# A hybrid attention layer in float32: weight splits in quarters, sums behind the value they delay, and two reorderings

## The chip, the cores and the metric

The kernel runs on one core of a Trainium2 chip (trn2). The metric is the device time of one launch in microseconds. The median of three runs is given, and one more execution was taken with the hardware profiler.

## The reference

One encoder layer on an input of 1024 tokens by 1024 features, all in float32:

```python
x = x + 0.5 * post1(SwiGLU_1(pre1(x)))                 # D_FF = 2816
h = mix_pre(x);  q, k, v = split(h @ w_qkv)            # 16 heads of 64
o_na  = neighbourhood_attention(q[:8], k[:8], v[:8])   # 16 x 64 token grid, window 8 x 16, learned bias
o_dil = dilated_mixture(q[8:], k[8:], v[8:])           # windows (128,1), (512,4), (2048,16), merged by their softmax sums
x = x + mix_post(concat(norm(o_na), norm(o_dil)) @ w_out)
x = x + 0.5 * post2(SwiGLU_2(pre2(x)))
# pre, post, norm: RMSNorm with a gain;  SwiGLU(h) = (silu(h @ w_gate) * (h @ w_up)) @ w_down
```

## The kernel before

**Precision.** Every float32 operand of a large matmul is split into two parts: `hi`, a copy cast to the matmul type fp32r by ScalarE, and `lo`, the float32 operand less `hi`, by VectorE. A product is then three matmuls: hi times hi, hi times lo and lo times hi. A matmul reads a stationary operand of 128x128 and streams a moving one of 512 columns into one of eight PSUM banks (2 KB per partition).

**Fewer products.** The GEMMs are done in a Strassen-Winograd form, seven products in place of eight, on sums and differences of blocks of the operands. The names A11, A12, S1 to S4, A22 stand for blocks or sums of the left operand, B11, B21, T1 to T4, B22 for those of the right one.

**The stages in order.** FFN1 (gate and up as pairs of columns in `PairGemm`, then the down projection in `Passes`); the projection of v (`Passes`) and of q and k (`PairGemm`); four pairs of dilated heads (`DilPair`, pairs 4 to 7); four pairs of neighbourhood heads (`na_head`); the output projection (`nat_mm`); FFN2, built as FFN1.

**PairGemm.run** goes over blocks of weights b. In an early block, whose first two products were made before, it computes S2 with T2 (and adds the stored `s1`, giving `u2`, L601), then the last product of the block before (A22), then S1 with T1 (adding u2 gives `v`, L609), S3 with T1 into another bank `d` (adding v gives `c22`, L628), and S4 with B22, which accumulates onto the bank of S1 that v has just read. The weights of block b + 1 are prepared beside it by the four steps of `prepare(b + 1)`: `direct` forms the sums and differences of the raw weights (L553, L554), `second` splits T2 (L456 on ScalarE, L457 on VectorE), `sums` splits T1 and forms one more difference (L561), and `rest` splits B22 and fetches the raw weights of block b + 3. `mm` is the product itself (L466, L467: hi with hi and lo; L472: lo with hi).

**Passes.run** goes over seven passes. `fetch` loads raw operands and splits them (L746 on ScalarE, L747 on VectorE, first the left side where it isn't resident in SBUF, then the right); L779 issues the matmuls of a product, for two blocks at a time in the first row tile and one at a time in the others.

**DilPair.head** goes over a head's four quads, each two units (eight units a head). A unit is four score matmuls (L1159), two reductions of scores plus bias by VectorE (L1066), two exponentials by ScalarE (L1068), and later the transposes of the unit three back (L1076), the copy of these into SBUF (`pt`, L1078, on VectorE or ScalarE by turns) and the products with the values of the unit four back (L1180). In the heads of pairs 6 and 7 the split of one tile of output weights of 1024 columns is put between (`Weights.steps`, L127 on ScalarE and L128 on VectorE). Its last part asks SyncE's queue for the next raw tile (`fetch`), of which there are two buffers.

**GroupNorm** normalizes the heads' outputs: `scaled(i)` multiplies one row block by its reciprocal root and the gain (L1342), `put(i)` transposes it (L1353, into one of two PSUM tiles) and splits it in two halves (L1357, L1358). The eight puts of the neighbourhood heads ("strip") go between the matmuls of the first stretch of the output projection.

**What sets the order.** TensorE runs in the order in which the program is written. On the other engines a planner orders the instructions by its own costs, those written first having precedence among those that are ready; an instruction issued inside `behind(f, engines)` comes after the last one written so far for each engine named. Each engine runs its instructions strictly in the planned order and waits for semaphores of other engines.

Of the kernel before, what the change touches and what calls it, by code (L numbers as in the profile page):

```python
# [16 lines left out]
SP, POOL, DVE, ACT = [getattr(mybir.EngineType, e) for e in ("SP", "Pool", "DVE", "Activation")]  # L17
# [7 lines left out]
NP = 4  # L25
# [160 lines left out]
class Operand:  # L186
# [10 lines left out]
    def second(self):  # L197
        for b in (S1, S2, S3, S4, A22):
            self.x[b] = [self.c.xb.tile([P, 4, T], F32R, tag=f"x{b}{i}", name=f"x{b}{i}") for i in range(2)]
# [232 lines left out]
class PairGemm:  # L432
# [151 lines left out]
    def run(self, final=None):  # L584

        c, nc, sp = self.c, self.c.nc, self.c.sp
        last = None
        if self.s1 is None:
            self.load_first()
        for b in range(self.n):  # L590
            w, early = self.w.pop(b), b < self.early
            direct, second, sums, rest = self.prepare(b + 1)
            if early:
                s1 = self.s1
                if b:
                    s1 = sp.tile([P, T], F32, tag="s1", name="s1")
                    nc.sync.dma_start(s1, self.kept[b])
                a = self.bank()
                self.mm(a, w[T2], 0, S2)
                u2 = sp.tile([P, T], F32, tag="u2", name="u2")  # L600
                nc.vector.tensor_add(u2, a, s1)  # L601
                if last:
                    last()
                self.c.behind(direct, *(self.sink.ties if b else (DVE,)))
                second()
                a = self.bank()
                self.mm(a, w[T1], 0, S1)
                v = sp.tile([P, T], F32, tag="v", name="v")
                nc.vector.tensor_add(v, a, u2)  # L609
            else:  # L610
                a = self.bank()
                self.mm(a, w["g"], 0, A11)
                s1 = self.keep(a, "s1")
                if last:
                    last()
                self.mm(a, w[T2], 0, S2, True)
                u2 = self.keep(a, "u2")
                pb = self.bank()
                self.mm(pb, w["g"], 1, A12)
                self.sink.first(b, pb, False, s1)  # L620
                self.tied(direct)
                second()
                self.mm(a, w[T1], 0, S1, True)
                v = self.keep(a, "v")
            d = self.bank()
            self.mm(d, w[T1], 1, S3)
            c22 = c.cp.tile([P, T], F32, tag="g2", name="c22", bufs=self.sink.deep)
            nc.vector.tensor_add(c22, d, v)  # L628
            self.sink.third(b, c22)
            sums()  # L630
            self.mm(a, w[B22], 0, S4, True)
            if final and b == self.n - 1 and self.sink.soon:
                final = final()
                c.behind(lambda: self.sink.second(b, a, u2 if early else None), DVE)
            else:
                self.sink.second(b, a, u2 if early else None)

            def last(b=b, d=d, w=w, u2=u2, c22=c22, rest=rest):
                self.mm(d, w[B22], 1, A22, True)
                c21 = c.cp.tile([P, T], F32, tag="c", name="c21")  # L640
                c.behind(lambda: nc.vector.tensor_add(c21, d, u2), *((DVE,) if self.sink.soon and b == self.n - 1 else ()))  # L641
                rest()
                self.sink.last(b, c21, c22, final)
            c.tick()
        if not self.sink.soon:
            final()
        last()
# [68 lines left out]
class Passes:  # L716
# [39 lines left out]
    def run(self, *which, upto=6):  # L756

        c = self.c
        for p in which:
            chained = PASSES[p][0] in CHAINED  # L760
            if not chained:
                self.acc = [None] * 4
            acc, groups = self.acc, self.groups[p]
            for gi, g in enumerate(groups):
                self.fetched(len(g) + 1, upto)
                ops = [self.ready.popleft() for _ in g]
                end = gi == len(groups) - 1
                for t in range(4):
                    if t == 1:
                        self.fetched(3, upto)  # L770
                    if acc[t] is None:
                        acc[t] = c.psm.tile([P, T], F32, tag="mm", name="accp")
                    sl = slice(t * P, (t + 1) * P)
                    n = 2 if t == 0 else 1
                    for j in range(0, len(ops), n):
                        two = [(a[:, sl], b) for i in (0, 1, 2) for (ahi, alo), (bhi, blo) in ops[j:j + n]
                               for a, b in [((ahi, bhi), (ahi, blo), (alo, bhi))[i]]]
                        for i, (a, b) in enumerate(two):
                            c.nc.tensor.matmul(acc[t], a, b, start=not chained and gi == 0 and j == i == 0,  # L779
                                               stop=end and j + n >= len(ops) and i == len(two) - 1,  # L780
                                               skip_group_check=chained)
                        if n == 2 or j % 2:
                            c.step()
                    if end:
                        self.take(p, t, acc[t])
                    c.tick()
# [295 lines left out]
class DilPair:  # L1082
# [28 lines left out]
    def head(self, hd, st, q, g, late, parts=(1, 0), more=(), begun=0):  # L1111
        more = deque(more)
        for i, (part, quad) in enumerate((part, quad) for part in parts for quad in range(2)):
            if (part, quad) == (0, 1):
                late()
            if i >= begun:
                self.quad(hd, st, q, g, part, quad, mid=(more, 1 - i) if i < 2 and more else ())

    def begin(self, st, g):

# [240 lines left out]
def layer(tc, a, out):  # L1361
    nc = tc.nc
    c = Ctx(tc)
    with ExitStack() as ctx:
# [10 lines left out]
        def ordered(*more):  # L1375
            return tc.manual_schedule(engines={mybir.EngineType.PE, *more})
# [464 lines left out]
        early = []  # L1841
# [8 lines left out]
        with ordered():  # L1850
            ops = sub()
            c.op = pool("op", 2, ops)
            c.vp.append(c.op)

            def next_ready():

                if loaded:
                    d, st, g = loaded[0]
                    if isinstance(d, DilPair):
                        qs.append(q_by_residue(c, nc.gpsimd.tensor_copy, st))  # L1860
                        by_residue(nc.gpsimd.tensor_copy, g[:, 0], g[:, 2])
            for p in range(NP, 2 * NP):
                for hd in range(2):
                    d, st, g = next_head(2 * (p - NP) + hd)
                    if (p, hd) == (NP + 1, 0):
                        queued(lambda: [c.w.fetch() for _ in range(2)] + [load_gains()])
                    if hd == 0:
                        d.outputs()
                    d.head(hd, st, qs.popleft(), g, next_ready, (1, 0) if p > NP or hd else (0, 1),
                           c.w.steps(2) if p > NP + 1 else (), (p, hd) == (NP, 0))  # L1870
            c.left = 64
            for p in range(NP):
                for hd in range(2):
                    vs, st, nb = next_head(8 + 2 * p + hd)
                    if (p, hd) == (NP - 1, 1):
                        c.todo.append(most)
                    na_head(c, p, hd, og[0], vs, st, nb, next_ready, last if (p, hd) == (NP - 1, 1) else lambda q: None)
            c.last_units()
            c.fill(len(c.fillers))
            c.tick(len(c.todo))  # L1880
            on = [c.xt.tile([P, 2, 4, T], F32R, tag=f"o{h}", name=f"n{h}") for h in (0, 2)]
            puts = deque()
            for quad, n in enumerate(early):
                n.ot = on
                for i in range(4):
                    if quad and i < 3:
                        puts.append(lambda i=i, n=n: (c.behind(lambda: n.scaled(i + 1), DVE), n.put(i)))
                    elif not quad and i == 0:
                        puts.append(lambda n=n: (n.put(0), c.behind(lambda: early[1].scale(1), DVE)))
                    else:  # L1890
                        puts.append(lambda i=i, n=n: n.put(i))
        s5.close()
# [3 lines left out]
        with ordered():  # L1896
            part, ws, od = [xo[k] for k in ("part", "ws", "dil")]
# [112 lines left out]
```

## Time and profile before

| | |
|---|---|
| Median of 3 runs | 1836.84 us (1836.69 to 1837.46) |
| Profiled execution | 1835.18 us |
| Its span, first to last instruction | 1833.0 us |
| Granted TensorE clock, mean | 0.999 |
| Busy: TensorE, VectorE, ScalarE, GpSimdE | 1813.7, 1321.5, 836.4, 324.1 us |
| Share of the chain that ended last | TensorE 93%, VectorE 3%, ScalarE 1%, DMA 1% |

In a row of the timeline the columns are the start in us, the duration in us, the engine, the line of the kernel, the operation, the tile written and those read, the count of instructions merged, and in brackets how long the engine stood idle before it and what ended the wait. In the view of waits they are the total in us, the number of waits and the longest. In the groups by line the two numbers behind the first bar are the busy time in us and the mean duration of one in ns, and behind the second bar the idle time before. Matmuls overlap, so their durations add up to more than the time that passes; TensorE's pace is read from the differences of its starts. PE is TensorE, DVE VectorE, ACT ScalarE, POOL GpSimdE, SP SyncE.

### The profile page before, as it was taken

To read this page: it belongs to the slowest core of one execution; us is meant where nothing else is said; L and a number is where in the kernel's file an instruction comes from. 1 tells how busy PE (TensorE), PEld (TensorE's weight loads), DVE (VectorE), ACT (ScalarE), POOL (GpSimd) and SP (SyncE) were. 2 spreads that over 40 slices of the span, in tenths; PEclk is the share of its full clock that TensorE was granted. 3 is DMA by queue.
4 is the path that set the end of the run, shared out by engine and by line. 5 is a ranking of instruction groups with operands and counts; after the bars stand their busy time and mean duration, and the time that the engine had idled before them with its cause. 6 is when DMAs were issued, how large, how long until landed. Compare 5 with 4: busy or idle time off the path is not lost.

```text
span 1833.0 us, 25132 instructions
## 1 busy us (share of the span) xinstructions
PE 1813.7 (99%) x8904; PEld 1525.8 (83%) x8904; DVE 1321.5 (72%) x2243; ACT 836.4 (46%) x1479; POOL 324.1 (18%) x508
## 2 busy tenths in 40 slices
PE   8999999999999999999999999999999999999998
PEld 6887888888888888888999998888888888888886
DVE  6878876776466877578677856788887777654557
ACT  6622233334444656234788765564223333354433
POOL 2123111112021133132333100121111111110000
PEclk9999999999999999999999999999999999999999
DMA  7756466557888868778686523594555566596564
GB/s 282 266 173 219 160 227 222 203 207 263 311 302 299 287 206 269 254 232 291 195 285 217 189 101 107 185 317 167 191 170 208 188 226 223 184 339 211 189 229 146
DMA packets 172991, 409.66 MB, mean 223 GB/s; under 512 B 20081, under 2 KB 42513, under 8 KB 170818
## 3 DMA queue, kind: packets, MB, share of 16 engines
q1 hardware_dynamic: 124706, 246.33, 40.6%
q0 software_dynamic: 47152, 159.64, 23.9%
q10 hardware_dynamic: 1008, 2.10, 0.3%
q8 instruction: 70, 1.15, 0.3%
q14 instruction: 55, 0.45, 0.1%
HBM read 280.49 MB, written 132.56 MB: 225 GB/s over the span
## 4 chain that ended last, share of the span: by engine, by line
PE 93%; DVE 3%; ACT 1%; issue 1%; DMA 1%; POOL 0%; SPq 0%; DVEq 0%; POOLq 0%; ACTq 0%
PE accp L779 27%; PE mmp L467 17%; PE mmp L466 17%; PE mmp L472 17%; PE po L1180 2%; PE po L1293 2%; PE ptp L1076 2%; PE accp L357 1%; PE accp L359 1%; PE accp L358 1%; PE trp L174 1%; PE sp L1277 1%; PE sp L1159 1%; ACT pb L1068 1%; DVE pt L1078 0%
## 5 line engine op out<-in xcount | busy, mean ns | idle before, releaser
L466 PE MATMUL mmp<-x,whi 128*128 128x512 f32 (+1 forms) x1464 | 571.9, 391 | 2.3 <-ACT x L181 1.3
L467 PE MATMUL mmp<-x,whi 128*128 128x512 f32 (+1 forms) x1464 | 569.7, 389 | 0.7 <-DVE x L182 0.6
L779 PE MATMUL accp<-pw 128*128 128x512 f32 x1800 | 411.0, 390 | 0.0
L779 PEld LDWEIGHTS accp<-pw 128*128 128x128 f32 x1800 | 337.3, 188 | 69.7
L472 PE MATMUL mmp<-x,wlo 128*128 128x512 f32 (+1 forms) x1464 | 390.5, 389 | 0.0
L466 PEld LDWEIGHTS mmp<-x,whi 128*128 128x128 f32 x1464 | 275.6, 188 | 60.8 <-ACT x L181 2.2
L467 PEld LDWEIGHTS mmp<-x,whi 128*128 128x128 f32 x1464 | 275.8, 188 | 57.3 <-DVE x L182 1.5
L472 PEld LDWEIGHTS mmp<-x,wlo 128*128 128x128 f32 x1464 | 274.6, 188 | 56.6
L747 DVE TENSOR_TENSOR pw<-praw,pw 128x1024 fp32r<-128x1024 f32 (+1 forms) x181 | 199.7, 1144 | 125.0 <-ACT pw L746 124.3
L746 ACT CAST pw<-praw 128x1024 fp32r<-128x1024 f32 (+1 forms) x181 | 168.5, 982 | 207.6 <-PE accp L779 165.6
L456 ACT CAST whi<-wraw 128x1024 fp32r<-128x1024 f32 x126 | 132.6, 1052 | 179.7 <-PE mmp L467 165.3
L457 DVE TENSOR_TENSOR wlo<-wraw,whi 128x1024 fp32r<-128x1024 f32 x126 | 153.9, 1223 | 2.7 <-ACT whi L456 2.7
L689 POOL DMA_DIRECT2D g<-sg x44 | 23.9, 543 | 430.8 <-DVE sg L682 243.0
L456 ACT CAST whi<-traw 128x512 fp32r<-128x512 f32 x52 | 32.3, 620 | 134.7 <-DVE traw L554 83.2
L641 DVE TENSOR_TENSOR c<-mmp,u 128x512 f32<-128x512 f32 x52 | 36.0, 692 | 76.6 <-PE mmp L472 76.4
L481 ACT COPY s<-mmp 128x512 f32<-128x512 f32 x52 | 30.6, 588 | 131.4 <-PE mmp L472 121.3
L553 DVE TENSOR_TENSOR wraw<-wraw 128x1024 f32<-128x1024 f32 x52 | 63.6, 1224 | 12.6 <-DMA wraw<-in_wu_dram 11.8
L779 PE MATMUL accp<-pw,x 128*128 128x512 f32 x312 | 72.0, 391 | 0.4 <-DVE pw L747 0.4
L779 PEld LDWEIGHTS accp<-pw,x 128*128 128x128 f32 x312 | 58.4, 188 | 12.9 <-DVE pw L747 0.8
L628 DVE TENSOR_TENSOR c<-mmp,v 128x512 f32<-128x512 f32 x52 | 35.8, 689 | 36.9 <-PE mmp L472 31.7
L1293 PE MATMUL po<-vs,pt 128*128 128x128 f32 x352 | 49.9, 276 | 0.0
L1076 PE MATMUL ptp<-ident,pb 128*128 128x128 f32 x304 | 48.8, 272 | 0.0
(273 smaller groups left out, 2489.0 us busy)
## 6 DMA issues: line engine op xcount, KB each, us to landing
praw<-g SPq DMA_DIRECT2D x70, 512.0 KB, 5.6
wraw<-in_wg_dram SPq DMA_DIRECT2D x44, 512.0 KB, 4.2
wraw<-in_wu_dram SPq DMA_DIRECT2D x44, 512.0 KB, 7.2
tr<-in_wd_dram SPq DMA_DIRECT2D x44, 512.0 KB, 6.8
g<-sg POOLq DMA_DIRECT2D x88, 256.0 KB, 5.2
ts<-tr POOLq DMA_DIRECT2D x22, 1024.0 KB, 4.7
praw<-ts SPq DMA_DIRECT2D x88, 256.0 KB, 4.0
praw<-in_wd_dram SPq DMA_DIRECT2D x66, 256.0 KB, 5.9
```

Source lines behind the costliest of these rows:

```text
L456: nc.scalar.copy(hi, raw)
L457: nc.vector.tensor_sub(lo, raw, hi.bitcast(F32))
L466: mm(out, hi[:, i, sl], xhi[:, k, cols], start=not go_on and k == 0, stop=False, skip_group_check=go_on)
L467: mm(out, hi[:, i, sl], xlo[:, k, cols], start=False, stop=False, skip_group_check=go_on)
L472: mm(out, lo[:, i, sl], xhi[:, k, cols], start=False, stop=k == 3, skip_group_check=go_on)
L553: nc.vector.tensor_sub(r[:, 0:2], r[:, 1:3], r[:, 0:2])
L746: nc.scalar.copy(hi, raw[:, :m])
L747: nc.vector.tensor_sub(lo, raw[:, :m], hi.bitcast(F32))
L779: c.nc.tensor.matmul(acc[t], a, b, start=not chained and gi == 0 and j == i == 0, stop=end and j + n >= len(ops) and i == len(two) - 1, sk ...
L1076: nc.tensor.transpose(ps[:, j, :], src[:, j * P:(j + 1) * P], c.ident)
L1180: nc.tensor.matmul(po[:, un * 2 + j], pt[:, 2 * j + t, :], rhs, start=t == 0, stop=t == 1)
L1293: nc.tensor.matmul(po[0][:, u], pt[0][:, j, :], vs[:, k0 + j, :], start=j == 0, stop=j == n - 1)
```

## The change

Four edits. In `PairGemm.run`, for the first block only, the steps `direct` and `second` of the second block are written behind v, and `direct` is ordered behind v's instruction on VectorE; before, they were written ahead of the product S1, `direct` ordered behind what VectorE had then. In `Passes.run` the three matmuls of a product go hi-hi, lo-hi, hi-lo (left part named first) instead of hi-hi, hi-lo, lo-hi. In `DilPair.head` the split of a weight tile goes in four parts of 256 columns, one to each quad (ahead of units 1, 2, 5 and 6), instead of two parts of 512 to the first two quads (ahead of units 1 and 2). In the output projection's puts the second quad's first two scalings are done at once, behind the first quad's first put, and the third and fourth each a put earlier.

```diff
                 if last:
                     last()
-                self.c.behind(direct, *(self.sink.ties if b else (DVE,)))
-                second()
+                if b:
+                    self.tied(direct)
+                    second()
                 a = self.bank()
                 self.mm(a, w[T1], 0, S1)
                 v = sp.tile([P, T], F32, tag="v", name="v")
                 nc.vector.tensor_add(v, a, u2)
+                if not b:
+                    self.c.behind(direct, DVE)
+                    second()
...
-                               for a, b in [((ahi, bhi), (ahi, blo), (alo, bhi))[i]]]
+                               for a, b in [((ahi, bhi), (alo, bhi), (ahi, blo))[i]]]
...
-                self.quad(hd, st, q, g, part, quad, mid=(more, 1 - i) if i < 2 and more else ())
+                self.quad(hd, st, q, g, part, quad, mid=(more, (i + 1) % 2) if more else ())
...
-                           c.w.steps(2) if p > NP + 1 else (), (p, hd) == (NP, 0))
+                           c.w.steps(4) if p > NP + 1 else (), (p, hd) == (NP, 0))
...
                 for i in range(4):
-                    if quad and i < 3:
-                        puts.append(lambda i=i, n=n: (c.behind(lambda: n.scaled(i + 1), DVE), n.put(i)))
+                    if quad and i < 2:
+                        puts.append(lambda i=i, n=n: (c.behind(lambda: n.scaled(i + 2), DVE), n.put(i)))
                     elif not quad and i == 0:
-                        puts.append(lambda n=n: (n.put(0), c.behind(lambda: early[1].scale(1), DVE)))
+                        puts.append(lambda n=n: (n.put(0), c.behind(lambda: early[1].scale(2), DVE)))
```

## The prediction, made before the changed kernel was run

> **What bounds the kernel now.** I read the page first: the span and TensorE's share of it.
>
> ```profile
> span 1833.0 us, 25132 instructions
> PE 1813.7 (99%) x8904; PEld 1525.8 (83%) x8904; DVE 1321.5 (72%) x2243; ACT 836.4 (46%) x1479; POOL 324.1 (18%) x508
> ```
>
> TensorE is busy for all but 19.3 us, most of that at the two ends. No edit takes a matmul away, so the only thing to gain is time in which TensorE stands still, and the only way to lose is to make it stand longer. The view of the waits on TensorE's side names where it stands away from the ends:
>
> ```profile
> PE mmp L466 <- DVE v L609: 1.0, 1, 1.0
> PE trp L1353 <- DVE og L1342: 0.9, 2, 0.5
> PE po L1180 <- DVE pt L1078: 0.7, 3, 0.3
> PE po L1180 <- ACT s L1068: 0.6, 2, 0.3
> PE accp L779 <- DVE pw L747: 0.4, 1, 0.4
> ```
>
> Each of the four edits meets one of these (the two rows of po L1180 are one place). They add up to only 3.6 us, but a wait also empties the pipeline of matmuls, so I measured each place by the spacing of TensorE's own starts, in the timeline, and those losses are larger.
>
> **Dilated heads' splits in four parts.** The starts of six consecutive heads:
>
> ```profile
> 929.71 0.72 PE L1159 MATMUL sp<-st,q 128*128 128x256 f32 x4
> 944.16 0.72 PE L1159 MATMUL sp<-st,q 128*128 128x256 f32 x4
> 959.25 0.37 PE L1159 MATMUL sp<-st,q 128*128 128x256 f32 x1
> 974.64 0.72 PE L1159 MATMUL sp<-st,q 128*128 128x256 f32 x4
> 989.73 0.72 PE L1159 MATMUL sp<-st,q 128*128 128x256 f32 x4
> 1005.13 0.48 PE L1277 MATMUL sp<-st 128*128 128x256 f32 x2
> ```
>
> The head from 929.71 has no split in it and takes 14.45 us (eight units of 1.81). The four after it each carry one split of a weight tile in two halves and take 15.09, 15.39, 15.09 and 15.40: 0.64 + 0.94 + 0.64 + 0.95 = 3.17 us of loss. How a half makes the loss, in the second of them:
>
> ```profile
> 961.76 0.60 ACT L127 CAST whi<-wraw 128x512 fp32r<-128x512 f32 x1
> 962.51 0.68 DVE L128 TENSOR_TENSOR wlo<-wraw,whi 128x512 fp32r<-128x512 f32 x1
> 963.12 0.42 DVE L1066 CUSTOM_DVE_ANT_0 s<-sp,g 128x256 f32<-128x256 f32 x1
> 963.46 0.69 DVE L1078 COPY pt<-ptp 128x512 f32<-128x512 f32 x1
> 964.29 1.13 PE L1180 MATMUL po<-va,pt 128*128 128x128 f32 x8 [0.28 <-ACT s L1068]
> ```
>
> VectorE runs without a hole from the split's subtraction L128 through a softmax's reduction L1066 to the copy pt, and pt ends at 964.15, just ahead of the product that reads it (the ScalarE instruction that the row names was long done). The half at the next unit does the same again: two stalls a head, 0.32 us each in the heads that lost 0.64 and 0.47 in those that lost 0.95. A quarter is 256 columns wide. The nearest rows of that width:
>
> ```profile
> L1358 DVE TENSOR_TENSOR n<-trp,n 128x256 fp32r<-128x256 f32 x16 | 6.7, 422 | 2.4 <-ACT n L1357 2.4
> L1357 ACT CAST n<-trp 128x256 fp32r<-128x256 f32 x16 | 5.7, 374 | 11.5 <-DVE n L1358 6.6 <-PE trp L1353 4.8
> ```
>
> So a quarter's subtraction takes 0.42 instead of 0.68, and pt comes 0.26 us earlier at each stall: 0.06 and 0.21 are left of 0.32 and 0.47. Four stalls of each kind: 4 x (0.06 + 0.21) = 1.08 left, 2.09 gained. The other two quarters go to units 5 and 6 of the head, where so far there is no split. VectorE has room there:
>
> ```profile
> 969.99 0.42 DVE L1066 CUSTOM_DVE_ANT_1 s<-sp,g 128x256 f32<-128x256 f32 x1 [0.92 <-PE sp L1159]
> 973.60 0.42 DVE L1066 CUSTOM_DVE_ANT_1 s<-sp,g 128x256 f32<-128x256 f32 x1 [0.93 <-PE sp L1159]
> ```
>
> It stood idle for 0.92 us before unit 5's reductions and 0.93 before unit 7's, waiting for TensorE's scores; two quarters need 0.84. I take them as hidden there. If they are not, they cost up to 8 x (0.37 + 0.42) = 6.3 us, ScalarE's cast and VectorE's subtraction one behind the other; if everything fits, the gain is the full 3.17. The fetch that follows a split goes out on SyncE's queue with the last part, some four units (7.2 us) later than now; the tile is wanted a head (15 us) on, and what then stands ahead of it in that queue are loads for the next pair, which come earlier for it. I cost it at nothing; a landing late by more than 7 us would stall the next split.
>
> By the rows, 1024 columns cost ScalarE 4 x 0.37 = 1.5 us in quarters against 2 x 0.60 = 1.2 in halves, and VectorE 4 x 0.42 = 1.7 against 2 x 0.68 = 1.4; what counts is that each piece is shorter where it stands in the way. The Trainium skill, "VectorE: DVE Perf Modes", section on the TRN2 errata, says that both engines pay a fixed latency per instruction and advises tiles of at least 512 elements, which halves keep and quarters break; from its formulas I would estimate 0.40 us for a quarter's cast and 0.42 for its subtraction. The trace agrees with these sizes, so the sum is the same by either; only the advice says otherwise, and what it would mean here is the second rival.
>
> **Left low products ahead of right.** One place shows a wait:
>
> ```profile
> 726.67 0.61 PE L779 MATMUL accp<-pw,x 128*128 128x512 f32 x2
> 727.66 2.14 PE L779 MATMUL accp<-pw,x 128*128 128x512 f32 x8 [0.38 <-DVE pw L747]
> 444.45 174.80 PE accp L779 x771
> 1266.93 0.91 PE mmp L472 x4
> ```
>
> The third matmul was due 2 x 0.227 behind 726.67, at 727.12, and came at 727.66: 0.54 lost to the weights' low half. With the operand's low half multiplied first, four matmuls stand ahead of it and it is due at 727.58: 0.08 is left, 0.46 gained. The order also breaks pairs of matmuls that share their stationary operand. The third row has 771 matmuls of which two in three share: 0.2267 us each. The fourth has four with an operand each: 0.2275. The difference would be 0.6 us over these 771 and some 1.7 over all of L779's, which are about three times as many, but the starts are rounded to 0.01; I take zero and keep 1.7 for the range.
>
> **Sums of the second block's weights behind v.** This acts in the first block of each of the three paired GEMMs. In the last one, FFN2:
>
> ```profile
> 1260.84 0.68 DVE L601 TENSOR_TENSOR u<-mmp,s 128x512 f32<-128x512 f32 x1
> 1261.44 1.22 DVE L553 TENSOR_TENSOR wraw<-wraw 128x1024 f32<-128x1024 f32 x1
> 1262.69 0.69 DVE L554 TENSOR_TENSOR traw<-wraw 128x512 f32<-128x512 f32 x1
> 1262.81 1.07 PE L472 MATMUL mmp<-x,wlo 128*128 128x512 f32 x4
> 1263.49 0.62 ACT L456 CAST whi<-traw 128x512 fp32r<-128x512 f32 x1 [3.83 <-DVE traw L554]
> 1264.02 0.68 DVE L609 TENSOR_TENSOR v<-mmp,u 128x512 f32<-128x512 f32 x1
> 1264.85 0.47 PE L466 MATMUL mmp<-x,whi 128*128 128x512 f32 x1 [0.97 <-DVE v L609]
> 1267.68 0.39 PE L466 MATMUL mmp<-x,whi 128*128 128x512 f32 x1
> ```
>
> The product S4 adds onto the bank that holds S1's, and v reads that bank in between, so S4 waits for v. The row at 1262.81 closes S3; a product of 12 matmuls takes 2.72 us, so S3 ended at 1263.72 and S1 at 1261.00. v could have run behind u at 1261.44; instead L553, L554 and L561 stood ahead of it. S4 should have begun at 1263.72 and ended at 1266.44; it ended at 1267.68: 1.24 us lost. With the sums behind v, v ends near 1262.1 and S4 finds it done: the whole 1.24, which I round to 1.2. What is queued behind v now: L553 from 1262.1, L554 at 1263.3, ScalarE's cast of T2 at 1264.0 instead of 1263.49, its low half by 1265.4. The next block's first product wants T2 at 1266.44, so a margin of a microsecond stays. In the other two GEMMs v was in time:
>
> ```profile
> 787.90 0.68 DVE L609 TENSOR_TENSOR v<-mmp,u 128x512 f32<-128x512 f32 x1
> 789.94 0.39 PE L466 MATMUL mmp<-x,whi 128*128 128x512 f32 x1
> ```
>
> In the q/k GEMM S4 begins at 789.94, S1 ended two products' starts earlier, at 787.22. There the edit only makes the sums wait: v at 787.3, then 1.22 + 0.69 + 0.62 + 0.69 of sum, difference, cast and low half: T2 ready near 791.3 where the next block begins one product behind 789.94, at 792.66. FFN1 has the same order and margin. I take no cost; without that margin it would be up to 1 us in each.
>
> **Strip norm's scalings one put ahead.** In the output projection's first stretch:
>
> ```profile
> 1126.50 0.63 PE L1353 MATMUL trp<-ident,og 128*128 128x128 f32 x4 [0.41 <-DVE og L1342]
> 1130.29 0.42 DVE L1358 TENSOR_TENSOR n<-trp,n 128x256 fp32r<-128x256 f32 x1 [0.44 <-ACT n L1357]
> 1130.63 0.74 DVE L1342 SCALAR_TENSOR_TENSOR og<-og,y,gd 128x512 f32<-128x512 f32 x1
> 1131.52 0.63 PE L1353 MATMUL trp<-ident,og 128*128 128x128 f32 x4 [0.53 <-DVE og L1342]
> ```
>
> The wait at 1126.50 is for the first scaling, which is as late as before. That at 1131.52 is for the fourth (1130.63 to 1131.37), which now comes a put earlier. But then L1358 of the put before is what is late: a put's transposes take one of two PSUM tiles, freed only by the second L1358 of the put two back, and a scaling of 0.74 moved ahead of it pushes 1130.71 to about 1131.2. So 0.2 to 0.6 of the 0.53 and its refill comes back; I take 0.3, and -0.2 as the bad end.
>
> **The sum.** 2.1 + 1.2 + 0.5 + 0.3 = 4.1 us. Nothing behind these places can swallow it: from the FFN2 start to the end TensorE's starts run at their spacing, so what is gained there and before moves the end. The profiled execution took 1835.18 us, 2.18 beyond its span; the runs' median is 1836.84. The profile should fall to about 1831.1, the median to 1832.7.
>
> **The rivals.**
> First, the quarters give back what they gain: ScalarE is busy with the units' exponentials, so a cast comes behind them, the in-order VectorE stands at L128, and new stalls as long as the remaining ones (1.1 us) appear there; or one of the small edits yields nothing. The gain is then 4.1 - 1.1 = 3.0, down to 1.9: 1834.4, within 0.2% of before (3.7 us, about what a measurement of this kernel can tell from no change). For it: each piece pays its fixed cost again. Against: the idle 0.92 and 0.93.
> Second, slower. The old stalls stay, because the pieces' order on VectorE and not their length made them, and all eight new quarters are exposed at 0.37 + 0.42 in units 5 and 6: 6.3 - 2.0 from the other edits = 4.3 slower, 1841.1. It decides if VectorE's idle time there falls before the cast is done rather than after. The Trainium skill's advice against tiles under 512 elements ("VectorE: DVE Perf Modes", same section) speaks for this one.
> Third, the sums behind v do not do what they say: T2 of the second block comes late in FFN2 and the wait moves from S4 to the next product: 1.2 less, 1833.9.
>
> **How the numbers follow.** Forecast 0.62 (own range 1830.5 to 1833.1), first rival 0.20, third 0.10, second 0.08. Faster by over 0.2% is the forecast: 0.62. Within: 0.20 + 0.10 = 0.30. Slower: 0.08. The low end of the range is every loss recovered, 3.17 + 1.24 + 0.54 + 0.9 or so, less a remainder: 1830.5; the high end leaves out only the second rival: 1837.0.
>
> **What would show it.** Right: heads of about 14.7 us between 944 and 1005; no wait on v L609 in FFN2, with v directly behind u; the wait on pw L747 under 0.1; four L127 and four L128 of 256 columns in each of the four heads. Wrong: new waits of po L1180 in the second half of those heads; a wait of mmp on a cast or low half of T2 in a second block; a mean spacing of L779's matmuls over 0.227; DVE og L1342 or a PSUM tile still holding the last put by 0.5.

## The result, and the profile after

The changed kernel takes 1832.60 us (median of 19 runs, 1831.38 to 1835.54) where the kernel before, run beside it, takes 1836.51 (19 runs, 1835.64 to 1838.58). The ratio is 0.9979, with a 95% interval of 0.9973 to 0.9985: faster by 3.9 us, 0.21% (2.8 to 5.0 us by the interval). The profiled execution took 1833.65 us. (Four lines were added to the file ahead of the loops, so that L779 is L783 in the rows below, L609 is L610, L1180 is L1184, and so on; L127 and L128 stand where they stood.)

The head of the page after, and from the view of TensorE's waits the rows that answer to those of before:

```profile
span 1831.5 us, 25146 instructions
PE 1814.0 (99%) x8904; PEld 1526.9 (83%) x8904; DVE 1321.9 (72%) x2251; ACT 835.6 (46%) x1487; POOL 322.5 (18%) x508
...
PE po L1184 <- DVE pt L1082: 0.8, 3, 0.3
PE trp L1357 <- DVE og L1346: 0.4, 1, 0.4
```

The waits for v and for pw are gone, and of the two for og one is left, the first scaling's. The row for pt is still there; the longest of its three waits, 0.34 us at 896, lies ahead of the four heads and is in both traces. Eight more VectorE and eight more ScalarE instructions are the extra pieces of the splits.

Because TensorE executes the same 8904 matmuls in both kernels, in the same order but for the low products, the starts can be compared one by one. Stage by stage, after less before, in us:

| stage (times of before) | first 30 | 30 to 444 | 444 to 620 | 620 to 726 | low products, 726 | dilated heads, 944 to 1005 | puts, 1118 to 1134 | FFN2's first blocks, 1258 to 1270 |
|---|---|---|---|---|---|---|---|---|
| after less before | +1.24 | +0.19 | +0.52 | +0.48 | -0.49 | -1.54 | -0.80 | -1.24 |

No stage left out differs by more than 0.04. The four places that were changed give 4.07 us together. The first four columns are not the change's work: `only_scalings` (below), whose edit touches none of these stages, showed +1.08, +0.08, -0.04 and +1.21 in them, and `eighths`, with all four edits and a finer split, +0.03, +0.38, -0.03 and -0.01. What makes these stages vary stays open. The execution profiled before was a quick one: its 1835.18 us lie under all of the 19 runs of that kernel. So the profiled time fell by only 1.53 us where the medians differ by 3.9.

**v in FFN2**, from the timeline after:

```profile
1260.38 0.68 DVE L601 TENSOR_TENSOR u<-mmp,s 128x512 f32<-128x512 f32 x1
1261.17 0.69 DVE L610 TENSOR_TENSOR v<-mmp,u 128x512 f32<-128x512 f32 x1
1261.78 1.22 DVE L553 TENSOR_TENSOR wraw<-wraw 128x1024 f32<-128x1024 f32 x1
1263.41 0.39 PE L466 MATMUL mmp<-x,whi 128*128 128x512 f32 x1
1264.10 0.62 ACT L456 CAST whi<-traw 128x512 fp32r<-128x512 f32 x1
1265.83 1.23 DVE L553 TENSOR_TENSOR wraw<-wraw 128x1024 f32<-128x1024 f32 x1 [2.11 <-DMA wraw<-in_wu_dram]
1266.13 0.39 PE L466 MATMUL mmp<-x,whi 128*128 128x512 f32 x1
1266.97 0.68 DVE L457 TENSOR_TENSOR wlo<-traw,whi 128x512 fp32r<-128x512 f32 x1
1267.94 1.07 PE L472 MATMUL mmp<-x,wlo 128*128 128x512 f32 x4
```

v now follows u and ends at 1261.86; S4 begins at 1263.41, directly behind S3, and the next product 2.72 later. T2's low half is the close one: it ends at 1267.65 and is read at 1267.94. It is that late because VectorE, in order, stood 2.11 us at the L553 of a later block, whose weights had not landed. In the trace of before, T2's low half stood ahead of that L553 (L457 at 1264.62, L553 at 1266.42).

**The low products**, timeline after, and then the pace of L783 (L779 before) in the chain that ended last, after and before:

```profile
728.28 1.07 PE L472 MATMUL mmp<-x,wlo 128*128 128x512 f32 x4
729.19 2.19 PE L783 MATMUL accp<-pw,x 128*128 128x512 f32 x8
```
```profile
1614.45 209.51 PE accp L783 x924
```
```profile
1616.00 209.48 PE accp L779 x924
```

Eight matmuls start without a gap. The 924 of the last stretch take 0.2267 us each in both orders.

**The puts**, timeline after:

```profile
1126.12 1.42 DVE L1346 SCALAR_TENSOR_TENSOR og<-og,y,gd 128x512 f32<-128x512 f32 x2
1127.02 0.63 PE L1357 MATMUL trp<-ident,og 128*128 128x128 f32 x4 [0.41 <-DVE og L1346]
1127.78 0.74 DVE L1346 SCALAR_TENSOR_TENSOR og<-og,y,gd 128x512 f32<-128x512 f32 x1
1128.18 0.60 PE L1357 MATMUL trp<-ident,og 128*128 128x128 f32 x4
1129.22 0.76 DVE L1362 TENSOR_TENSOR n<-trp,n 128x256 fp32r<-128x256 f32 x2 [0.36 <-ACT n L1361]
1129.89 0.74 DVE L1346 SCALAR_TENSOR_TENSOR og<-og,y,gd 128x512 f32<-128x512 f32 x1
1130.12 0.63 PE L1357 MATMUL trp<-ident,og 128*128 128x128 f32 x4
1130.55 0.42 DVE L1362 TENSOR_TENSOR n<-trp,n 128x256 fp32r<-128x256 f32 x1
1131.28 0.60 PE L1357 MATMUL trp<-ident,og 128*128 128x128 f32 x4
```

The four puts are 1.16, 1.94 and 1.16 us apart where they were 1.16, 2.00 and 1.86. The fourth scaling (1129.89) stands between the two L1362 of the put of 1128.18; that tile is free at 1130.97, and the fourth put, at 1131.28, waits neither for the scaling nor for the tile.

**The heads.** The starts of the same six, and then the second of the four from the inside:

```profile
931.74 0.48 PE L1163 MATMUL sp<-st,q 128*128 128x256 f32 x2
946.19 0.48 PE L1163 MATMUL sp<-st,q 128*128 128x256 f32 x2
960.75 0.48 PE L1163 MATMUL sp<-st,q 128*128 128x256 f32 x2
976.11 0.36 PE L1163 MATMUL sp<-st,q 128*128 128x256 f32 x1
990.65 0.48 PE L1163 MATMUL sp<-st,q 128*128 128x256 f32 x2
1005.63 0.48 PE L1281 MATMUL sp<-st 128*128 128x256 f32 x2
```
```profile
963.26 0.40 ACT L127 CAST whi<-wraw 128x256 fp32r<-128x256 f32 x1
963.40 0.25 DVE L1225 RECIPROCAL dn<-dn 128x16 f32<-128x16 f32 x1
963.70 0.43 DVE L128 TENSOR_TENSOR wlo<-wraw,whi 128x256 fp32r<-128x256 f32 x1
964.90 0.69 DVE L1082 COPY pt<-ptp 128x512 f32<-128x512 f32 x1
965.73 1.13 PE L1184 MATMUL po<-va,pt 128*128 128x128 f32 x8 [0.21 <-DVE pt L1082]
966.17 0.42 DVE L128 TENSOR_TENSOR wlo<-wraw,whi 128x256 fp32r<-128x256 f32 x1
966.23 2.13 POOL L1237 TENSOR_TENSOR obn<-obn,w 128x1024 f32<-128x1024 f32 x1
970.37 2.08 POOL L1059 CAST q<-st 128x1024 fp32r<-128x1024 f32 x1
971.83 0.91 DVE L128 TENSOR_TENSOR wlo<-wraw,whi 128x256 fp32r<-128x256 f32 x1
972.66 0.68 DVE L1082 COPY pt<-ptp 128x512 f32<-128x512 f32 x1
973.39 1.16 PE L1184 MATMUL po<-vb,pt 128*128 128x128 f32 x8
```

The heads take 14.56, 15.36, 14.54 and 14.98 us beside 14.45 of one without a split: 0.11, 0.91, 0.09 and 0.53 lost, 1.64 in all, where 3.17 were lost. (The 1.53 gained is the table's 1.54 but for rounding.) The first heads of a pair are all but clean. In the second heads the quarter at unit 1 still costs 0.45 (the wait at 965.73 and the refill behind it) and the next one 0.08; in this one the third quarter costs another 0.38 at 973.39, because its L128 took 0.91 us where its neighbours take 0.42. That instruction ran beside GpSimdE's cast of q for the next head.

### The profile page after: what moved, and what is told of

Read it like the earlier page. It is cut to its first block, busy times and chain, and to the rows that moved or that the text cites. A ratio compares the mean times of both kernels' runs of the same rounds, so it can differ in the third digit from the quotient of the medians.

```text
span 1831.5 us, 25146 instructions
## 1 busy us (share of the span) xinstructions
PE 1814.0 (99%) x8904; PEld 1526.9 (83%) x8904; DVE 1321.9 (72%) x2251; ACT 835.6 (46%) x1487; POOL 322.5 (18%) x508
## 4 chain that ended last, share of the span: by engine, by line
PE 80%; issue 11%; DMA 3%; DVE 3%; ACT 2%; POOL 1%; SPq 0%; POOLq 0%; DVEq 0%; ACTq 0%
PE accp L783 24%; PE mmp L466 14%; PE mmp L467 14%; PE mmp L472 14%; PE po L1184 3%; PE ptp L1080 2%; PE po L1297 2%; PE accp L357 1%; PE accp L359 1%; PE accp L358 1%; PE sp L1163 1%; PE trp L174 1%; PE sp L1281 1%; POOL g L717 1%; ACT pb L1072 1%
## 5 line engine op out<-in xcount | busy, mean ns | idle before, releaser
L783 PE MATMUL accp<-pw 128*128 128x512 f32 x1800 | 411.2, 390 | 0.3 <-ACT hb L804 0.3
L783 PEld LDWEIGHTS accp<-pw 128*128 128x128 f32 x1800 | 337.2, 188 | 70.5 <-ACT hb L804 0.7
L457 DVE TENSOR_TENSOR wlo<-wraw,whi 128x1024 fp32r<-128x1024 f32 x126 | 153.1, 1217 | 2.3 <-ACT whi L456 2.3
L553 DVE TENSOR_TENSOR wraw<-wraw 128x1024 f32<-128x1024 f32 x52 | 63.6, 1224 | 18.5 <-DMA wraw<-in_wu_dram 17.8
L783 PE MATMUL accp<-pw,x 128*128 128x512 f32 x312 | 71.8, 390 | 0.0
L783 PEld LDWEIGHTS accp<-pw,x 128*128 128x128 f32 x312 | 58.3, 188 | 12.3 <-DVE pw L751 0.4
```

The costliest lines, as they stand in the source:

```text
L457: nc.vector.tensor_sub(lo, raw, hi.bitcast(F32))
L553: nc.vector.tensor_sub(r[:, 0:2], r[:, 1:3], r[:, 0:2])
```

## The experiments

**The four edits, one at a time.** Each is one hunk of the diff applied to the kernel before.

```diff
only_v:          direct and second of the second block written behind v
only_low:        ((ahi, bhi), (alo, bhi), (ahi, blo))
only_quarters:   mid=(more, (i + 1) % 2), c.w.steps(4)
only_scalings:   scaled(i + 2) for i < 2, early[1].scale(2)
```

> The kernel before with one edit: sums of the second block's weights behind v. Theory (v is what S4 waits for): the wait of mmp on v in FFN2's first block (0.97 us idle, 1.24 us lost) goes wholly, the profile has no other new wait in a second block, and the median falls by 1.2 us (0.07%). Rival (the wait only moves on): the next product waits for T2 instead, and the median stays within 0.3 us of before.

> The kernel before with one edit: the left low product ahead of the right one in the passes. Theory: the third matmul's wait at 727 us shrinks from 0.38 to under 0.1, 0.46 us are gained there, and the pace of the passes' matmuls stays at 0.2267 us: 0.5 us less in all (0.03%, at the edge of what the runs can tell). Rival (matmuls that no longer share their stationary operand are slower): the pace rises to 0.2275 and the median by 1.2 us (1.7 less 0.5).

> The kernel before with one edit: the splits of the dilated heads in quarters. Theory (a shorter piece stands a shorter time in the way): the four heads lose about 1.6 us together as in the changed kernel, against 3.17 before, so 1.5 us less (0.08%). Rival (each piece's fixed cost counts): losses in units 5 and 6 make up for it and the median stays within 0.3 us of before.

> The kernel before with one edit: the strip norm's scalings one put ahead. Theory of the prediction (a PSUM tile takes the scaling's place as what is late): 0.3 us less. Rival (the scaling alone was late): the spacing of the second quad's four puts goes back to 1.14, 1.82 and 1.14, and 0.8 to 0.9 us are gained, as the changed kernel's trace suggests (0.79 less lost between 1120 and 1140 us).

| kernel | median, us (before: 1836.52) | ratio, 95% interval | its own place in the trace, us |
|---|---|---|---|
| only_v | 1835.75 | 0.9995 (0.9986 to 1.0004) | -1.22 |
| only_low | 1836.34 | 1.0000 (0.9991 to 1.0009) | -0.49 |
| only_quarters | 1835.07 | 0.9993 (0.9984 to 1.0002) | -1.79 |
| only_scalings | 1835.79 | 0.9995 (0.9986 to 1.0004) | -0.80 |

No single edit can be told from nothing by its time: each interval holds 1. The traces can tell them, because the low products, the heads and the puts repeat to 0.03 us where an edit is absent, and FFN2's first blocks to 0.24. Each edit acts where it was placed. In their own places the first three came as expected, and `only_scalings` gave the 0.8 of its rival and not the 0.3 of the prediction. The sum of the four medians' falls, 3.13, lies near the 3.91 of all together, which says little with an interval of 1.6 us to each side of every one. The quarters alone lose 0.10, 0.67, 0.10 and 0.52 in the four heads, 1.39 of TensorE's time. Here the third quarter of the second head took 0.67 us and not 0.91, because GpSimdE's cast beside it had begun 0.27 us earlier within the head.

**Is it the length of a piece, or its place?** Two kernels with all four edits vary the split: halves in units 5 and 6, where VectorE stood idle, and eighths, one in each unit. (The lines that pass the list of units on to `quad` are left out here.)

```diff
 halves_late
-   c.w.steps(4) if p > NP + 1 else (), (p, hd) == (NP, 0))
+   c.w.steps(2) if p > NP + 1 else (), (p, hd) == (NP, 0), (5, 6))
 eighths
+   c.w.steps(8) if p > NP + 1 else (), (p, hd) == (NP, 0), range(8))
```

> The changed kernel with the dilated heads' splits in two halves of 512 columns again, but ahead of units 5 and 6, where the new quarters went, and none ahead of units 1 and 2. Theory of the prediction (VectorE's idle 0.9 us before units 5 and 7 hides what stands there; the place matters as much as the size): the four heads lose at most 1.6 us together. Rival (ScalarE's exponentials fill units 5 and 6, so that a cast of 0.60 us pushes them late; only the small size saves the quarters): the heads lose 2.5 us or more together, as the halves in the old place did with 3.17.

> The changed kernel with the splits in eight parts of 128 columns, one ahead of each unit. Theory (the piece's length in the way makes the stall): pieces of about 0.29 us on either engine lose less than the quarters' 1.64 us in the four heads, 0.5 to 1.2. Rival (each piece pays its fixed cost again, about 0.15 on VectorE and 0.2 on ScalarE, so eight of them crowd engines that have little room): as much or more than the quarters, 1.6 to 3.

Both lose more in the heads than the quarters, and more than their theories allowed; the eighths lose more than their rival allowed, too. The halves took 1838.04 us and lost 4.55 us in the heads, with another 1.14 in the stretch behind them; the eighths took 1841.43 and lost 11.45. These are single executions, and the halves' time lies within the spread of the kernel before beside it (1836.01 to 1838.37), so what follows goes by the traces. The timeline of the halves, first head, and a row of TensorE's waits in that kernel:

```profile
956.37 2.06 POOL L1059 CAST q<-st 128x1024 fp32r<-128x1024 f32 x1
956.43 2.56 DVE L128 TENSOR_TENSOR wlo<-wraw,whi 128x512 fp32r<-128x512 f32 x1
...
960.33 0.94 PE L1184 MATMUL po<-vb,pt 128*128 128x128 f32 x6 [1.46 <-DVE pt L1082]
...
PE po L1184 <- ACT pt L1082: 1.5, 2, 0.8
```

and of the eighths, first head:

```profile
952.69 1.41 POOL L1059 COPY g<-g 128x384 f32<-128x384 f32 x1 [8.82 <-PE ptp L1080]
953.29 0.97 DVE L128 TENSOR_TENSOR wlo<-wraw,whi 128x128 fp32r<-128x128 f32 x1
954.05 2.14 POOL L1059 CAST q<-st 128x1024 fp32r<-128x1024 f32 x1
954.87 1.48 DVE L128 TENSOR_TENSOR wlo<-wraw,whi 128x128 fp32r<-128x128 f32 x1
```

A subtraction of 512 columns, 0.69 us elsewhere, took 2.56; two of 128 columns, 0.29 elsewhere, took 0.97 and 1.48. Each began while a GpSimdE instruction ran, and ended 0.56, 0.15 and 0.15 us behind that instruction's end, which is its usual duration less 0.13 to 0.14: it did not run slowly, it stood ready, waited and then ran. In the eighths eight of the 32 were caught, for 8.06 us beyond 0.29 each. TensorE's units behind them are some 9.9 us longer than 1.81 each, most of the 11.45 lost. The fixed cost of twice as many pieces was not separated from this.

GpSimdE is not the whole account of the halves. Two of the eight were caught (the other took 1.37 us), and the units behind them are 2.25 us longer, about half of the 4.55. The rest stands where no L128 was lengthened; its largest waits are those of the last row, 0.63 us in these heads and 0.85 behind them, for copies pt that ScalarE makes. What makes those late was not taken apart, so for this half the rival, a cast that pushes ScalarE's work back, is not ruled out. In any case VectorE's idle time before units 5 and 6 was a poor guide: GpSimdE is at work in it.

**Around the additions, then around the casts.** Three placements of the four quarters, in the second heads of the pairs:

```diff
 moved
+   (3, 4, 6, 7) if hd else (1, 2, 5, 6)
 free_1
+   ((1, 4, 6, 7) if p == 6 else (1, 4, 5, 6)) if hd else (1, 2, 5, 6)
 free_0
+   ((0, 4, 6, 7) if p == 6 else (0, 4, 5, 6)) if hd else (1, 2, 5, 6)
```

> The changed kernel with the quarters of the second head of a pair ahead of units 3, 4, 6 and 7 instead of 1, 2, 5 and 6, away from the small operations that merge the pair before (first units) and from GpSimdE's cast of q, beside which one subtraction took 0.91 us instead of 0.42. Theory (VectorE's fullness in the first units makes what is left, 0.91 and 0.53 us in these heads): they lose at most 0.3 each, and about 0.8 us are gained on the changed kernel. Rival (ScalarE is the tighter engine in units 3 to 7): they lose 0.5 or more each, nothing is gained. A subtraction with both operands in SBUF that overlaps a GpSimdE operation should end about 0.28 us behind that operation's end, if the two exclude each other.

> The changed kernel with the quarters of the second heads placed by GpSimdE's free time: ahead of units 1, 4, 6 and 7 in pair 6, of 1, 4, 5 and 6 in pair 7. Theory (what is left comes from one full VectorE stretch at units 1 and 2, and from subtractions that GpSimdE shuts out): the four heads lose 0.7 us or less together, against 1.64 in the changed kernel and 0.95 with units 3, 4, 6, 7; no wait of 0.5 us comes in the first neighbourhood head, where unit 7's quarter in pair 7 left one; the median is 0.5 to 1 us under the changed kernel's 1832.6. Rival (ScalarE in units 4 to 7 is what counts): the second heads lose 0.4 or more each, nothing is gained.

> As the run beside it, with unit 0 in place of unit 1 in both second heads. Theory: VectorE stands idle for 0.6 us ahead of unit 0's reductions in the changed kernel's second head of pair 6, so the quarter costs even less there: 0.5 us or less lost in the four heads. Rival (the cast comes behind the head before's exponentials on ScalarE, and VectorE waits for it in order): more than with unit 1, 0.8 to 1.5 us.

| kernel | lost in the four heads, us | behind them, us | median, us | ratio to before, 95% interval |
|---|---|---|---|---|
| after | 0.11, 0.91, 0.09, 0.53 | 0.02 | 1832.60 | 0.9979 (0.9973 to 0.9985) |
| moved | 0.10, 0.35, 0.14, 0.36 | 0.60 | 1832.24 | 0.9974 (0.9963 to 0.9984) |
| free_1 | 0.11, 0.46, 0.14, 0.46 | 0.02 | 1832.38 | 0.9974 (0.9963 to 0.9984) |
| free_0 | 0.09, 0.25, 0.14, 0.25 | 0.05 | 1832.20 | 0.9974 (0.9964 to 0.9984) |

`moved` only moved the loss: its second heads lost a little over the 0.3 expected, but its waits have a new row, behind the heads. Two of its four lengthened quarters, 0.94 us each, ran beside GpSimdE's additions. All four ended 0.28 or 0.29 us behind the GpSimdE instruction beside them, as its expectation had it.

```profile
PE po L1297 <- DVE pt L1082: 0.5, 1, 0.5
```

`free_1` lost clearly more than was expected of it. By its number, 0.46 in each second head, its rival is met, but not by its mechanism: the whole loss stands behind unit 1's quarter, where TensorE takes 2.26 us for a unit, and from unit 3 on every unit takes 1.81, though the quarter at 969.19 was lengthened to 1.04 us beside the copy of g. So a lengthened piece need not cost TensorE anything. `free_0` lost somewhat more than was expected, though the least of all: with the first quarter a unit earlier, its cast stands ahead of the unit's exponentials on ScalarE, and the wait for pt near 965 falls from 0.21 us to under 0.02. By its trace `free_0` beats the changed kernel by 0.9 us in the heads; the times, 0.4 us apart, do not tell the two from each other.

**Taking GpSimdE's copies away.** To see whether GpSimdE is what holds L128, the cast of q and the copy of g of the next head go to ScalarE in the two kernels that suffered most:

```diff
-   qs.append(q_by_residue(c, nc.gpsimd.tensor_copy, st))
-   by_residue(nc.gpsimd.tensor_copy, g[:, 0], g[:, 2])
+   qs.append(q_by_residue(c, nc.scalar.copy, st))
+   by_residue(nc.scalar.copy, g[:, 0], g[:, 2])
```

> The kernel with halves ahead of units 5 and 6, with GpSimdE's two copies for the next head (g, and the cast of q) given to ScalarE. Theory (GpSimdE and a VectorE subtraction with both operands in SBUF exclude each other): the two subtractions that took 2.56 and 1.37 us beside those copies take 0.69 like the other six, and TensorE's wait of 1.46 us in the first of the four heads goes; ScalarE's added 1.5 us a head may cost elsewhere. Rival (something else made them long, such as a late cast): they stay over 1 us.

> The kernel with the splits in eighths, with the same two copies given to ScalarE. GpSimdE's two products of the merge stay, in the second heads. Theory: the eighths beside the former copies (0.97, 1.48, 1.92 and 0.61 us) take 0.29; those beside the merge's products still take up to 2 us; the four heads lose clearly less than 11.45 us, 5 to 9. Rival (eight fixed costs are what crowds the heads): over 10.

The instructions of L128 in the heads' stretch, with their shortest, median and longest duration in ns: first with GpSimdE's copies, then without.

```profile
L128 DVE TENSOR_TENSOR wlo<-wraw,whi x8: 691/692/2556, 956.4 to 1006.9; 128x512 fp32r<-128x512 f32 x8
```
```profile
L128 DVE TENSOR_TENSOR wlo<-wraw,whi x8: 682/692/693, 979.9 to 1034.2; 128x512 fp32r<-128x512 f32 x8
...
PE po L1184 <- ACT pt L1082: 20.1, 8, 4.7
```

All eight halves are back at 0.69. In the eighths four of the eight lengthened ones are back at 0.29, those beside the copies; the four that remain stand beside the additions (L1237, L1238) that stayed on GpSimdE. One such pair of L128, in the timeline of those eighths:

```profile
986.66 2.19 DVE L128 TENSOR_TENSOR wlo<-wraw,whi 128x128 fp32r<-128x128 f32 x2
986.81 1.90 POOL L1238 TENSOR_TENSOR oa<-oa,w 128x1024 f32<-128x1024 f32 x1 [4.05 <-DVE w L1227]
```

The first of the pair began ahead of the addition and took 0.28; the second took 1.99. That settles what lengthens L128. As kernels the two are far slower (1866.72 and 1864.55 us): ScalarE needs 2.04 us for each cast and 0.90 for each copy, and it waits for their transfers in order, with the exponentials and the copies pt queued behind; in the first, TensorE's eight waits for pt from ScalarE make 20.1 us. They answer what holds L128, and not what the heads would take without it; what was expected of the heads' losses cannot be read from them.

## Why the prediction was right, and where its steps were not

- **The time.** 1832.7 was forecast, 1832.60 measured; the likeliest case came true. The time alone, with its 2.8 to 5.0 us, would also fit the third rival's gain of 2.9; it is the traces that rule that one out. The sum, 4.1 against 4.07 in the trace, owes its closeness to luck, two errors that cancel: the quarters gave 0.56 less than forecast and the scalings 0.50 more. The low end of the range does not follow from its own terms: 3.17 + 1.24 + 0.54 + 0.9 = 5.85 off 1836.84 gives 1831.0, and a remainder would raise it, so 1830.5 is too low.
- **Sums behind v: right in size.** 1.24 was read off the trace and 1.24 came (1.22 alone). The third rival, T2 late, did not come, and no second block shows a new wait. The step "a margin of a microsecond stays" is wrong for T2's low half: it was to end near 1265.4 and ended at 1267.65, 0.29 us before it was read. The step listed what is queued behind v in the order of before; in the new order a later block's L553 stands ahead of that low half, and waits for a transfer. (In the q/k GEMM, S1 ended one product ahead of S4's start and not two; the time given, 787.22, is right.)
- **Low products: right.** 0.46 forecast, 0.49 measured, alone and together; the broken pairs of shared operands cost nothing that the pace shows.
- **Scalings: the term was mis-sized, 0.3 against 0.80.** The step that failed is "a scaling of 0.74 moved ahead of it pushes 1130.71 to about 1131.2". It added the fourth scaling ahead of that L1358 and forgot that the third, which stood there before (1128.78), moves out by the same edit. In fact that tile is free 2.79 us behind its put's start, where it took 3.05 before and would have taken 3.5 by that step; the fourth scaling runs in part where VectorE stood waiting for ScalarE's cast before (the 0.44 us ahead of 1130.29). So the whole wait of 0.53 and its refill are gone, and `only_scalings` shows the same 0.80 by itself.
- **Quarters: mis-sized, 2.09 against 1.53.** "pt comes 0.26 us earlier at each stall" holds for the first heads: 0.12 left in each by the sum, 0.11 and 0.09 measured. In the second heads 0.42 was to be left and 0.91 and 0.53 were. Part of it, 0.11 in each, is a changed order on VectorE. The cast comes behind two exponentials on ScalarE in both kernels; before, VectorE had a reduction and two small products to do ahead of L128 (L1066 at 962.05, L1222, L1223), but in the changed kernel L128 stands ahead of these, and VectorE stood at it until the cast's end at 963.66 (0.30 from the start of L1225 to that of L128, where the instruction behind it began 0.17 later in the trace of before). So that stall fell by 0.07 instead of 0.26. The next one fell by 0.36: by the 0.26, and by about 0.09 by which GpSimdE had lengthened that half before (the row at 964.73 in the last section). The rest, 0.38 in one head, is the stall at 973.39 behind an L128 of 0.91 us. "I take them as hidden there" therefore failed for one of the eight quarters in units 5 and 6, and not for the reason weighed: VectorE had room, but could not use it while GpSimdE ran.
- **The rivals.** The first gets a part of its mechanism (VectorE standing at L128 for a cast behind the exponentials) and, by another cause, one new stall, 0.38, a third of its price. Of the second nothing came: halving the pieces did shorten the stalls, and the advice of the Trainium skill, "VectorE: DVE Perf Modes", section on the TRN2 errata, against tiles under 512 elements would have led the wrong way here, since what counted was the delay of the next instruction in an in-order queue. The eighths do not test that advice cleanly, as most of their loss stands behind pieces that GpSimdE held.
- **The listed signs.** Heads of about 14.7: two at 14.55, two above. No wait on v or on pw: so. New waits of po in the second half of those heads were to be a sign of something wrong, and one came. The profile's own time was to be near 1831.1 and was 1833.65, for the 2.43 us of the first four stages, which the forecast took as equal.

## What to carry to other kernels

Before you shorten or move work on VectorE into its idle time, look at what GpSimdE runs in that time: L128, a subtraction with both operands in SBUF, got no part of it while a GpSimdE instruction ran, however short it was. When an edit shifts a whole sequence by one place, take away what moves out as well as adding what moves in. And cut a piece where it stands ahead of something that another engine waits for, with its producer's queue checked too: the quarter was 0.26 us shorter, and worth 0.07 where VectorE came to it before its cast was done.

## What the runs showed of the hardware

**VectorE and GpSimdE exclude each other on some instructions.** L128 reads two operands from SBUF. Started while a GpSimdE instruction on SBUF runs, it ends a fixed time behind that instruction: 0.15 us for 128 columns, 0.28 for 256, 0.56 for 512, unless its usual time from its own start ends later (the quarter at 955.64 took 0.43 us, though the copy of g beside it ran until 955.73). Started first, it takes its usual time, and GpSimdE waits: the addition L1237 at 966.23 began beside a quarter and took 2.13 us, where it takes 1.90 at 937.0 and 1023.3, away from the splits. VectorE's reductions L1070, with one operand in PSUM, took their 0.42 us beside the cast of 970.37. The Trainium skill, "SBUF — State Buffer", section "Who interferes with whom", says that the second pair of SBUF ports is shared by the two engines as an exclusive lock, that a VectorE instruction with two SBUF inputs contends with a GpSimd instruction that reads SBUF, and that the order of issue decides which of the two blocks. Every one of these rows agrees with it, and the prediction, which did not weigh it, would have gained by it: of the eight quarters taken as hidden, the one that began beside the cast was not free. The trace of before had shown it, in the second half of the second head:

```profile
964.73 0.78 DVE L128 TENSOR_TENSOR wlo<-wraw,whi 128x512 fp32r<-128x512 f32 x1
```

The addition L1234 ran beside it from 962.66 to 964.96, and this half took 0.78 us, ending 0.55 behind the addition, where the half before it took 0.68.

**The first 30 us differ from run to run by as much as an edit brings.** The same stretch of the first matmuls, before and then after, with the count of matmuls in it:

```profile
15.00:18.00 3.00, 3.00 (x22) 2.52 (x21) 2.07 (x4) 2.56 (x6) 1.24 (x2) 1.00 0.23 87
```
```profile
15.00:18.00 3.00, 3.00 (x17) 3.00 (x15) 1.28 (x2) 1.89 (x4) 1.24 (x2) 1.00 0.21 79
```

TensorE is busy throughout in both, but starts 22 matmuls in one and 17 in the other: after their first few, matmuls start every 0.21 us, and from some moment on every 0.11 to 0.12. That moment comes near 15.3 us in the profile before and near 18.3 in the one after. The row's granted clock is 1.00 in both and does not show it. The Trainium skill, "TensorE: Matmul & The Clock Gate", section "What's actually happening" of its first part, says that the clock's warm-up follows a free-running window, so that the number of slow matmuls at a kernel's start varies from run to run; these rows fit that, and no run here shows the cause itself. With edits worth 0.5 to 1.5 us one should compare stages, not ends.
